# Where the convolution phases stand among the attention blocks: 15 ahead instead of 16, a first transform put behind the scores, three and two phases per attention step instead of two and one

## The chip, the core and the metric

The kernel runs on one core of a Trainium2 chip. The core has a matrix engine (PE, with its weight loads shown as PEld), a vector engine (DVE), a scalar engine (ACT), a general engine (POOL) and a queue engine (SP) that here only issues DMA transfers; POOL issues some as well. Each engine takes its instructions in a fixed order and waits at the head of its queue until what the head needs is there. The metric is the device time of one execution in microseconds (us). A change of less than 0.3% can hardly be told from none.

## What is computed

One layer of a diffusion backbone, in float32, on 1024 latent tokens and 256 context tokens. After a modulated normalisation one projection feeds two groups of heads: attention over a neighbourhood plus context keys, and a long convolution (Hyena) done by Fourier transforms. Both outputs are normalised, joined and put through one output projection; a convolutional feed-forward follows.

```python
proj = h @ w_in
q, k, v = ...                                  # 8 attention heads of width 64
a   = attend(q, k, v)                          # window + all context keys, one softmax
z   = x1 * _long_conv(v_h, k_f[:, 0], bias[0]) # Hyena: two convolutions in a row
hyo = x2 * _long_conv(z,   k_f[:, 1], bias[1])
x = x + g1 * (concat(rms(a), rms(hyo)) @ w_out)
u = dwconv3(h2 @ w_up); x = x + g2 * ((silu(gate) * up) @ w_down)
```

## The kernel before, in words

The program is one long stream, traced in Python and then put into an order for each engine by a scheduler, which takes instructions by priority (earlier traced is more urgent, and a block in `high_priority` more still) as their inputs become ready in its own estimate. The order is fixed when the kernel runs.

The stage that matters lies between the input projection and the output projection:

- **The convolution chains.** `chain(j)` is a generator for one block of 128 channels: blocks 0 to 3 are latent, block 4 is the context. It stops at eight `yield`s, four for each of the two convolutions `o`; what lies between two stops is a *phase*. Phase 0 is the forward transform: PE matmuls with `dftf` (L805), ACT scalings (L813 to L818) and DVE rotations (L819). Phase 1 is a butterfly (L826 to L831) and the product with the filter spectrum `K` (L844 to L847). Phase 2 is the inverse butterfly (L852 to L857) and rotations (ACT L862, L863, DVE L864). Phase 3 is the inverse transform (PE L877) and the gate (L882 to L884, or ACT L887 and DVE L888 to L890 in the second convolution), and in the second convolution the store of the result to `hyd` (L895, for the context block L898).
- **Two lanes.** Blocks 0, 2, 4 follow each other in lane 0, blocks 1 and 3 in lane 1. The list `turn2` says which lane gives the next phase: 0, 0, then 1 and 0 in turn. There are 40 phases in all. `phases(n)` traces the next n of them.
- **Ahead of the attention** 16 phases are traced with high priority: all eight of block 0, seven of block 1 and the first of block 2. They have three PSUM banks `cA`. Afterwards the chains have one bank, in the rest of the program.
- **The attention.** `attend(p_)` handles one pair of heads, four pairs in all. For each half `b` of the queries it computes the scores of two column blocks (PE L1068, DVE mask and maximum L1089, L1096, L1099, ACT exponentials L1102, L1103), stops, then sums (L1149), turns the weights around (PE L1112, copied out by ACT L1022 or DVE L1020), multiplies with the values (PE L1030) and normalises (PE L1040, L1045, DVE L1159). A pair stops three times. At the stops `phases(2)`, `phases(1)`, `phases(2)` are traced, and `phases(2)` at the end of a pair: five within a pair, seven with its end.
- **Bias tables** `tb` are filled by POOL's transfers (L967), 16 for each of three tables in each pair.
- **After the attention** `w_out` is loaded in nine pieces `wor` (L1205) into the memory that the chains leave, each split into a high and a low part (ACT L1197, DVE L1198), two or three pieces in flight. The attention output is split likewise (`ar`, ACT L1291, DVE L1292), the convolution output is read back as `y` (L1304), normalised (L1306, L1309), turned around (PE L1312) and split (`mr`, L1314, L1315). The output projection `psd` (L116 to L118, three matmuls for each product) takes `ar` for a block of 128 tokens first and `mr` after it, and the feed-forward follows.

Of the kernel before, what the change touches and what calls it, by code (L numbers as in the profile page):

```python
# [24 lines left out]
NH, DH = 8, 64  # L25
# [61 lines left out]
def _build(nc, tc, top, V, A, G, T, Q, I, O, dbg, upto):  # L87
# [20 lines left out]
    def bk(tag):  # L108
        pl, n, bufs = banks[tag]
        return pl.tile([P, 512 * n], F32, tag=tag, name="ps" + tag, bufs=bufs)  # L110
# [389 lines left out]
    with ies:  # L500
# [3 lines left out]
        for gi, (s, col, tl) in enumerate(groups):  # L504
            xs = []
# [24 lines left out]
            n = P * len(tl)  # L530
# [232 lines left out]
    dftf = cp.tile([P, 2, 256], F32, name="dftf")  # L763
    idft = cp.tile([P, 2, 2, P], F32, name="idft")
    with tc.high_priority(offset=2000):
        Q.dma_start(out=dftf.rearrange("p a b -> p (a b)"), in_=I["t_dft"].flatten().rearrange("(p x) -> p x", p=P))
        Q.dma_start(out=idft.rearrange("p a b c -> p (a b c)"), in_=I["t_idft"].flatten().rearrange("(p x) -> p x", p=P))

    S4B, TB = 3, 1
    CHP = 2000  # L770

    def chain(j):
# [22 lines left out]
        for o in range(2):  # L795
            uv = u.rearrange(v2, i=2)
            Gt = s8()
            Gv = Gt.rearrange(f4, h=2, i=2, q=4)
            for h in range(2):
                hs = slice(h * P, (h + 1) * P)  # L800
                for rp in range(2):
                    pa = bk("cA")
                    xs = slice(rp * 256, (rp + 1) * 256)
                    for i in range(2):
                        T.matmul(pa[:, i * 256:(i + 1) * 256], dftf[:, i, hs], uv[:, i, xs], start=True, stop=True)  # L805
                    pv = pa.rearrange("p (i r c) -> p i r c", i=2, r=2)
                    if not lat:
                        A.copy(Gv[:, h, :, 2 * rp:2 * rp + 2], pv)
                        continue
                    for ri in range(2):  # L810
                        r = 2 * rp + ri
                        if r == 0:
                            A.copy(Gv[:, h, :, 0], pv[:, :, 0])  # L813
                            continue
                        c, s, ns = tw_chain(h, r)
                        t = cp.tile([P, 2, P], F32, tag=f"t{b_}", name="t", bufs=TB)
                        A.activation(t[:, 0], pv[:, 1, ri], AF.Copy, scale=ns)
                        A.activation(t[:, 1], pv[:, 0, ri], AF.Copy, scale=s)  # L818
                        V.scalar_tensor_tensor(Gv[:, h, :, r], pv[:, :, ri], c, t, op0=ALU.mult, op1=ALU.add)  # L819
# [52 lines left out]
            for rp in range(2):  # L872
                pa = bk("cA")
                xs = slice(rp * 256, (rp + 1) * 256)
                for i in range(2):
                    for h in range(2):
                        T.matmul(pa[:, i * 256:(i + 1) * 256], idft[:, i, h], Ys[:, h, i, xs], start=h == 0,  # L877
                                 stop=h == 1, skip_group_check=True)
# [26 lines left out]
    def phases(n):  # L905
        for _ in range(n):
            if turn2:
                next(lanes[turn2.pop(0)], None)

    with tc.high_priority(offset=CHP):  # L910
        phases(16)
    cbk.close()
    cbk = Banks("bkd", "right", "tile", cA=(1, 1))
    for _ in ada:
# [137 lines left out]
    def attend(p_):  # L1052

        with tc.issue_after(blast0) if p_ == 1 else ExitStack():
            q, k = qkload(p_) if p_ else first
# [7 lines left out]
        hs = [slice(h * DH, (h + 1) * DH) for h in range(2)]  # L1063
        Pc = {}

        def smm(outs, qc, kc):
            for h in range(2):
                T.matmul(outs[h], q[hs[h], qc], kc(hs[h]), start=True, stop=True, tile_position=(DH * h, 0),  # L1068
                         skip_group_check=True)

        def scores(cb, l, l2, j):

            u0, u1 = BLK[cb]
            nu = u1 - u0
            a0 = 2 * cb - 1 + u0
            var = (0, 1, 1, 2)[cb]
            qc = [slice((2 * cb + half) * P, (2 * cb + half + 1) * P) for half in range(2)]
            m = [stat(f"m{h}") for h in range(2)]
            loc = [[], []]
            for half in range(2):  # L1080
                r0, nr = HALF_ROWS[half]
                n = nu * nr * 8
                sl = bk("S").rearrange("p (h x) -> p h x", h=2)
                smm([sl[:, h, :n] for h in range(2)], qc[half], lambda r: kg[r, a0:a0 + nu, r0 * 8:(r0 + nr) * 8])
                for h in range(2):
                    reg = Pring[h][cb][:, half, :, r0:r0 + nr].rearrange("p u r c -> p u (r c)")
                    loc[h].append(reg)
                    tv = tbs[var][:, HOFF[half]:HOFF[half] + nr * 64].rearrange("p (h u x) -> p h u x", h=2, u=4)[:, h]
                    V.tensor_tensor_reduce(out=reg, in0=sl[:, h, :n].rearrange("p (u x) -> p u x", u=nu),  # L1089
                                           in1=tv[:, u0:u1], op0=ALU.add, op1=ALU.max, scale=1.0, scalar=-3.0e38,  # L1090
                                           accum_out=m[h][:, half:half + 1])
            sc = bk("S").rearrange("p (h x) -> p h x", h=2)
            for half in range(2):
                smm([sc[:, h, half * 256:(half + 1) * 256] for h in range(2)], qc[half], lambda r: k[r, LT:])
            m2 = stat("n", 4)
            V.tensor_reduce(m2, sc.rearrange("p h (a x) -> p (h a) x", a=2), axis=AX.X, op=ALU.max, negate=True)  # L1096
            pc = tp.tile([P, 2, 2, 256], F32, tag="pc", name="pc", bufs=3)
            for h in range(2):
                V.scalar_tensor_tensor(m[h], m[h], -1.0, m2[:, 2 * h:2 * h + 2], op0=ALU.mult, op1=ALU.min)  # L1099
                for half in range(2):  # L1100
                    c = 4 * h + 2 * j + half
                    A.activation(loc[h][half], loc[h][half], AF.Exp, bias=m[h][:, half:half + 1], accum_out=l[:, c:c + 1])  # L1102
                    A.activation(pc[:, h, half], sc[:, h, half * 256:(half + 1) * 256], AF.Exp,  # L1103
                                 bias=m[h][:, half:half + 1], accum_out=l2[:, c:c + 1])
            Pc[cb] = pc
# [38 lines left out]
        for b in range(2):  # L1144
            l, l2 = stat("l", 8), stat("l2", 8)
            for j in range(2):
                scores(2 * b + j, l, l2, j)
            yield
            V.tensor_add(l, l, l2)  # L1149
            av = bk("av")  # L1150
            for j in range(2):
                cb = 2 * b + j
                for kt in range(2):
                    ps = turn(lambda h, i: Pc[cb][:, h, i, kt * P:(kt + 1) * P])
                    av_mm(av, 256 * j, vs[:, 10 + kt], ps, kt == 0)
                for vt, ps in local(cb):
                    av_mm(av, 256 * j, vt, ps, False)
            bs = recips(l, 8)
            V.tensor_mul(dst[:, 2 * b:2 * b + 2], av.rearrange("p (b r c) -> p b r c", b=2, r=16),  # L1159
                         bs.rearrange("p (b r c) -> p b r c", b=2, r=16))  # L1160
            if b == 0:
                yield
# [6 lines left out]

    for p_ in range(4):  # L1170
        for n, _ in enumerate(attend(p_)):
            phases(2 - n % 2)
        phases(2)
    ces.close()
    cbk.close()
# [407 lines left out]
    for f in range(NFF):  # L1583
# [7 lines left out]
        i, cs = f // 2, slice(f % 2 * 256, f % 2 * 256 + 256)  # L1591
# [132 lines left out]
    xs = {}  # L1724
# [107 lines left out]
```

## Time and profile before

| what | value |
|---|---|
| three runs | 1839.21, 1842.02 and 1844.18 us, median 1842.02 |
| the profiled execution, its own time | 1843.86 us |
| its span, from the first to the last instruction | 1841.9 us |
| busy share of the span: PE, DVE, ACT, POOL | 94%, 74%, 49%, 22% |
| mean granted PE clock | 0.964 of full speed |
| end of the last projection matmuls, start of the attention's scores | 562 us, 588 us |
| last normalisation of the attention (L1159) | 846.55 us |
| first matmul of the output projection | 861.32 us |

The profile is of one execution. A row of the timeline gives the start and the length of a group of equal instructions in us, the engine, the line of the kernel, what is written and read, and in brackets how long the engine had been idle before it and what ended that. The windows view gives for each stretch the busy time of PE, PEld, DVE, ACT and POOL with the count of instructions, the granted PE clock, the share of DMA time and the rate. The chain of waits follows the work that ended last back to its start. Busy times of PE overlap a little, as its matmuls are pipelined.

### The profile page before, as it was taken

What the parts mean: (1) busy time and instruction counts of PE and PEld (TensorE: products, weight loads), DVE (VectorE), ACT (ScalarE), POOL (GpSimd) and SP (SyncE); (2) the same over time, 40 slices, a digit from 0 to 9 for tenths busy, and PEclk for the clock granted to TensorE, in tenths of its full rate; (3) what the DMA queues carried; (4) which work ended last, traced back from release to release, by engine and by line L of the source; (5) the groups of instructions that cost most, each with busy time, mean ns of one, the idle gap of its engine ahead of it and who ended that gap; (6) DMA issues with size and microseconds to landing.
All of it is one profiled execution on the core that took longest, in us unless ns stands there. A gap on an engine that the chain in (4) does not pass through costs nothing.

```text
span 1841.9 us, 27359 instructions
## 1 busy us (share of the span) xinstructions
PE 1725.3 (94%) x9999; PEld 1453.2 (79%) x9999; DVE 1367.1 (74%) x2166; ACT 893.9 (49%) x1852; POOL 396.7 (22%) x487
## 2 busy tenths in 40 slices
PE   5899999999996898898997999999999999999997
PEld 1588788788884455566886999999999999888786
DVE  4658957853778798973558798889777877566797
ACT  4645535533334566664556444444444444443452
POOL 2266565674117442600110000000000000000001
PEclk7899999999997799998998999999999999999999
DMA  7424354356546332516231554454222123934653
GB/s 247 157 87 135 105 176 131 112 132 192 168 143 194 96 106 69 147 35 213 78 109 50 165 167 151 157 164 163 82 65 73 60 65 102 350 112 142 207 185 132
DMA packets 202440, 249.78 MB, mean 136 GB/s; under 512 B 21923, under 2 KB 147988, under 8 KB 202050
## 3 DMA queue, kind: packets, MB, share of 16 engines
q1 hardware_dynamic: 190360, 230.75, 38.8%
q0 software_dynamic: 10240, 16.46, 3.7%
q8 instruction: 79, 1.29, 0.3%
q10 hardware_dynamic: 1705, 0.82, 0.2%
q14 instruction: 56, 0.45, 0.1%
HBM read 176.75 MB, written 71.20 MB: 135 GB/s over the span
## 4 chain that ended last, share of the span: by engine, by line
PE 38%; DVE 14%; DMA 8%; issue 4%; ACT 3%; POOL 1%; DVEq 0%; POOLq 0%; ACTq 0%; SPq 0%
PE psd L116 6%; PE psd L117 6%; PE psd L118 6%; PE psa L116 3%; PE psa L117 3%; PE psa L118 3%; DMA wt<-in_w_down_dram 2%; PE psc L118 2%; PE psc L117 2%; PE psc L116 2%; PE psb L117 2%; PE psb L118 2%; PE psb L116 2%; DMA tdr<-wt 2%; POOL tb L967 1%
## 5 line engine op out<-in xcount | busy, mean ns | idle before, releaser
L116 PE MATMUL psp<-hh,wh 128*128 128x512 f32 (+1 forms) x552 | 200.6, 363 | 1.9 <-ACT wh L121 1.9
L118 PE MATMUL psp<-hh,wl 128*128 128x512 f32 (+1 forms) x552 | 199.5, 362 | 1.0 <-POOL wl L122 1.0
L117 PE MATMUL psp<-hl,wh 128*128 128x512 f32 (+1 forms) x552 | 198.9, 360 | 0.0
L1747 POOL TENSOR_TENSOR rs<-rs,mhalf 128x1 f32<-128x1 f32 x10 | 7.7, 776 | 816.0 <-DVE rs L1746 816.0
L116 PE MATMUL psa<-T,ws 128*128 128x256 f32 (+1 forms) x528 | 166.0, 314 | 3.9 <-ACT rows L1546 2.7
L117 PE MATMUL psa<-T,ws 128*128 128x256 f32 (+1 forms) x528 | 165.3, 313 | 0.0
L118 PE MATMUL psa<-T,ws 128*128 128x256 f32 (+1 forms) x528 | 164.7, 312 | 0.0
L116 PE MATMUL psd<-wd,gs 128*128 128x512 f32 x360 | 140.8, 392 | 3.1 <-ACT gs L121 3.1
L117 PE MATMUL psd<-wd,gs 128*128 128x512 f32 x360 | 141.0, 392 | 0.0
L118 PE MATMUL psd<-wd,gs 128*128 128x512 f32 x360 | 123.3, 390 | 1.7 <-DVE gs L122 1.6
L116 PEld LDWEIGHTS psp<-hh,wh 128*128 128x128 f32 x552 | 104.9, 190 | 23.2 <-issue 7.4
L118 PEld LDWEIGHTS psp<-hh,wl 128*128 128x128 f32 x552 | 104.9, 190 | 16.4 <-POOL wl L122 1.2
L117 PEld LDWEIGHTS psp<-hl,wh 128*128 128x128 f32 x552 | 104.8, 190 | 14.1 <-issue 0.4
L116 PE MATMUL psc<-T,ws 128*128 128x384 f32 (+1 forms) x352 | 110.1, 313 | 5.8 <-ACT ws L121 5.8
L118 PE MATMUL psc<-T,ws 128*128 128x384 f32 (+1 forms) x352 | 110.0, 313 | 0.3 <-DVE ws L122 0.3
L967 POOL DMA_DIRECT2D tb<-rpw x192 | 100.5, 531 | 45.1 <-DVE m L1089 31.7
L117 PE MATMUL psc<-T,ws 128*128 128x384 f32 (+1 forms) x352 | 110.1, 313 | 0.0
L117 PE MATMUL psb<-T,ws 128*128 128x384 f32 (+1 forms) x352 | 109.4, 311 | 0.0
L118 PE MATMUL psb<-T,ws 128*128 128x384 f32 (+1 forms) x352 | 109.4, 311 | 0.0
L116 PE MATMUL psb<-T,ws 128*128 128x384 f32 (+1 forms) x352 | 109.2, 310 | 0.0
L116 PEld LDWEIGHTS psa<-T,ws 128*128 128x128 f32 x528 | 101.4, 192 | 5.7 <-ACT rows L1546 4.0
L117 PEld LDWEIGHTS psa<-T,ws 128*128 128x128 f32 x528 | 101.3, 192 | 0.0
(405 smaller groups left out, 4785.8 us busy)
## 6 DMA issues: line engine op xcount, KB each, us to landing
wada<-in_w_ada_dram SPq DMA_DIRECT2D x48, 512.0 KB
wr<-in_w_up_dram SPq DMA_DIRECT2D x44, 512.0 KB
gr<-gdr SPq DMA_DIRECT2D x44, 320.0 KB
wr<-in_w_in_dram SPq DMA_DIRECT2D x23, 512.0 KB
wt<-in_w_down_dram SPq DMA_DIRECT2D x44, 256.0 KB
tdr<-wt SPq DMA_DIRECT2D x44, 256.0 KB
gdr<-cv SPq DMA_DIRECT2D x22, 512.0 KB
wr<-tdr SPq DMA_DIRECT2D x20, 512.0 KB
```

Source lines behind the costliest of these rows:

```text
L116: T.matmul(out, ah, bh, start=start, stop=False, skip_group_check=True)
L117: T.matmul(out, ah, bl, start=False, stop=False, skip_group_check=True)
L118: T.matmul(out, al, bh, start=False, stop=stop, skip_group_check=True)
L967: blast[0] = G.dma_start(out=tv[:, :, a * 8:a * 8 + 64], in_=rpw[var, :, 2 * p_:2 * p_ + 2, :, d * 8:d * 8 + 64].rearrange("q h u x -> q ( ...
L1747: G.tensor_tensor(rs, rs, mhalf, op=ALU.pow)
```

## The change

Three edits. `phases(16)` ahead of the attention becomes `phases(15)`, so the first phase of block 2 is traced within the attention, without high priority and on the single bank. A list `gate` holds the last scores matmul of the newest half block; from then on, each forward transform of a chain's first convolution (`o == 0`) is put behind that matmul in PE's order, by a constraint on the order that adds no semaphore. And the stops of a pair trace 3, 2 and 3 phases instead of 2, 1 and 2: eight within a pair where there were five, ten with its end where there were seven. 25 phases are left for the attention, so they are used up at the second stop of the third pair.

```diff
+    gate = []
@@ chain(j), phase 0
-                    for i in range(2):
-                        T.matmul(pa[:, i * 256:(i + 1) * 256], dftf[:, i, hs], uv[:, i, xs], start=True, stop=True)
+                    with tc.issue_after(gate[0]) if gate and o == 0 else ExitStack():
+                        for i in range(2):
+                            T.matmul(pa[:, i * 256:(i + 1) * 256], dftf[:, i, hs], uv[:, i, xs], start=True, stop=True)
@@
     with tc.high_priority(offset=CHP):
-        phases(16)
+        phases(15)
@@ smm, the scores matmuls
-                T.matmul(outs[h], q[hs[h], qc], kc(hs[h]), start=True, stop=True, tile_position=(DH * h, 0),
-                         skip_group_check=True)
+                smm.last = T.matmul(outs[h], q[hs[h], qc], kc(hs[h]), start=True, stop=True,
+                                    tile_position=(DH * h, 0), skip_group_check=True).ins
@@ attend, behind the scores of a half
+            gate[:] = [smm.last]
             yield
@@
         for n, _ in enumerate(attend(p_)):
-            phases(2 - n % 2)
+            phases(3 - n % 2)
         phases(2)
```

No instruction is added or taken away; what changes is where they stand. In the changed kernel a line number is two higher from the transform (L805 becomes L807) and three higher behind the gate (L1159 becomes L1162, L1205 becomes L1208).

The first place is PE's queue where the attention begins, behind the transposes of the cached keys (L732). Before, the eight transform matmuls of block 2 (L805) stand first, and the last phase of block 1 (L877) stands among the scores (L1068):

```order
L732 MATMUL pstB<-ident,ck 128x128 x2
L805 MATMUL pscA<-s_5771,dftf 128x256 x8
L1068 MATMUL psS<-k,q 128x264 x2
L1068 MATMUL psS<-k,q 128x288 x2
L877 MATMUL pscA<-s_5623,idft 128x256 x4
L1068 MATMUL psS<-k,q 128x256 x4
L1068 MATMUL psS<-k,q 128x352 x2
L877 MATMUL pscA<-s_5623,idft 128x256 x4
L1112 MATMUL psX<-ident,pc 128x128 x6
```

In the changed kernel the scores follow at once, and no chain matmul stands before the second block's last scores:

```order
L732 MATMUL pstB<-ident,ck 128x128 x2
L1070 MATMUL psS<-k,q 128x264 x2
L1070 MATMUL psS<-k,q 128x288 x2
L1070 MATMUL psS<-k,q 128x256 x4
L1070 MATMUL psS<-k,q 128x352 x2
L1114 MATMUL psX<-ident,pc 128x128 x6
...
L1070 MATMUL psS<-k,q 128x256 x4
L807 MATMUL pscA<-s_5969,dftf 128x256 x4
```

So the transform of block 2 moved behind the scores of the first half block, and the last phase of block 1, which shares its bank, moved behind that.

The second place is DVE at the same point. Before, the rotations of block 2 (`s_5773`), its butterfly and half of the rotations of block 1 (`s_5623`) stand ahead of the first mask (L1089, written as ISA):

```order
L819 SCALAR_TENSOR_TENSOR s_5773<-pscA,tw,t 128x2x128
L826 TENSOR_TENSOR s_6035<-s_5773 128x1024
L864 SCALAR_TENSOR_TENSOR s_5623<-s_5623,tw,t 128x2x128
L827 TENSOR_TENSOR s_5773<-s_5773 128x4x256
L830 TENSOR_TENSOR s_6036<-s_6035 128x4x128
L831 TENSOR_TENSOR s_6036<-s_6035 128x4x128
L1089 ISA Pl_5833,m_5950<-psS,tb_5857 128x3x88
```

In the changed kernel only rotations of block 1 are left there, and the maxima of the attention follow:

```order
L866 SCALAR_TENSOR_TENSOR s_5623<-s_5623,tw,t 128x2x128 x4
L1091 ISA Pl_5792,m_5909<-psS,tb_5816 128x3x88
L1091 ISA m_5909 128x1
L1091 ISA Pl_5796,m_5910<-psS,tb_5816 128x3x88
L1091 ISA m_5910 128x1
L866 SCALAR_TENSOR_TENSOR s_5623<-s_5623,tw,t 128x2x128 x2
L1098 TENSOR_REDUCE n<-psS 128x4
```

So all that block 2 had DVE do there has moved behind the first masks.

The third place is ACT's queue behind the attention. Before, the splits of all nine pieces of `w_out` stand ahead of the split of the attention output (L1291), mixed with the attention's last copies:

```order
L1197 ACTIVATE wh_8309<-wor,vec 128x1024
L1222 ACTIVATE sq<-at_5828 128x1024
L1197 ACTIVATE wh_8315<-wor,vec 128x1024
L1197 ACTIVATE wh_8321<-wor,vec 128x1024
L1197 ACTIVATE wh_8327<-wor,vec 128x512 x2
L1291 CAST ar<-at_5828 128x512 x2
```

In the changed kernel the last copies of the last chain phase (L889, before L887) stand behind all of the attention, and the attention output is split after four pieces:

```order
L1225 ACTIVATE sq<-at_5787 128x1024
L889 COPY tt<-pscA 128x256 x2
L1200 ACTIVATE w_8280<-wor,vec 128x1024 x2
L1200 ACTIVATE w_8281<-wor,vec 128x1024
L1200 ACTIVATE wh_8303<-wor,vec 128x1024
L1294 CAST ar<-at_5787 128x512 x2
L1200 ACTIVATE wh_8309<-wor,vec 128x1024
```

So the chains now end last in this stage, and the output projection needs four pieces instead of nine before it can begin. On SP's queue the reads of `y` (L1307) have likewise moved ahead of the last pieces of `wor`, behind the seventh of the nine.

## The prediction

> **What bounds the kernel now.** I read the windows view first. Its columns are the stretch, its length, the busy time of PE, PEld, DVE, ACT and POOL with their counts, the granted PE clock, the DMA share and GB/s.
>
> ```profile
> 576.40:618.00 41.60, 22.31 (x68) 13.93 (x68) 39.46 (x70) 16.93 (x61) 24.20 (x45) 0.66 0.74 214
> 631.60:846.50 214.90, 197.10 (x1227) 120.47 (x1228) 176.79 (x376) 140.73 (x433) 71.42 (x134) 0.98 0.34 96
> 640.00:680.00 40.00, 38.46 (x248) 23.25 (x246) 38.56 (x78) 26.82 (x85) 13.63 (x26) 1.00 0.39 112
> 861.30:900.00 38.70, 38.68 (x166) 31.28 (x167) 15.54 (x33) 17.06 (x33) 3.81 (x7) 0.93 0.48 164
> 1003.00:1600.00 597.00, 583.95 (x3823) 575.31 (x3823) 482.75 (x668) 267.76 (x425) 0.36 (x9) 0.99 0.40 129
> ```
>
> The limit changes from stage to stage. Where the attention begins (576 to 618) DVE binds: 39.46 of 41.60 us, with PE half idle. In the attention (631.6 to 846.5) PE is busy 91.7% of the time and DVE 82%; in its dense piece (640 to 680) both stand at 96%. Behind it PE binds alone (38.68 of 38.70, later 97.8%), so a shift of the output projection's start reaches the end unless a later wait takes it up. Next the chain of waits at the two seams (start, length, what).
>
> ```profile
> 577.37 5.65 DMA s<-lxd
> 583.07 2.09 PE pscA L805 x4
> ...
> 827.60 0.70 DVE s L890
> 828.32 2.78 DMA hyd<-s
> ...
> 831.17 3.40 DMA wor<-in_w_out_dram
> ...
> 861.32 0.79 PE psd L116
> ```
>
> At the first seam the end hangs on a load for block 2's transform. At the second it hangs on the **last gate of the chains**, L890: it lets `hyd` be stored and the memory for `w_out` go free. The attention's last row (L1159, at 846.55) is not on this chain.
>
> **The change, part one: the lead at the first seam.** The timelines of PE and DVE there:
>
> ```profile
> 575.82 0.64 PE L732 MATMUL pstB<-ident,ck 128*128 128x128 f32 x2
> 583.07 5.50 PE L805 MATMUL pscA<-s,dftf 128*128 128x256 f32 x16 [6.61 <-DMA s<-lxd]
> 588.49 1.20 PE L1068 MATMUL psS<-k,q 64*128 64x264 f32 x8
> ...
> 616.96 2.05 PE L805 MATMUL pscA<-s,dftf 128*128 128x256 f32 x4 [0.97 <-DMA s<-lxd]
> 618.93 1.12 PE L1030 MATMUL psav<-pt,vs 128*64 128x256 f32 x4
> ```
>
> ```profile
> 588.31 0.68 DVE L857 TENSOR_TENSOR s<-s 128x512 f32<-128x512 f32 x1
> ...
> 590.66 0.48 DVE L864 SCALAR_TENSOR_TENSOR s<-s,tw,t 128x256 f32<-128x256 f32 x1
> ...
> 591.91 0.48 DVE L864 SCALAR_TENSOR_TENSOR s<-s,tw,t 128x256 f32<-128x256 f32 x1 [0.16 <-ACT t L863]
> ...
> 598.07 0.42 DVE L1089 CUSTOM_DVE_ANT_0 Pl<-psS,tb 128x264 f32<-128x264 f32 x1
> ...
> 609.52 0.23 DVE L1099 SCALAR_TENSOR_TENSOR m<-m,n 128x2 f32<-128x2 f32 x2
> ...
> 631.60 0.17 DVE L1149 TENSOR_TENSOR l<-l,l 128x8 f32<-128x8 f32 x1 [0.66 <-ACT pc L1103]
> ```
>
> The first scores move from behind L805 to behind L732 and are done near 578 (576.46 plus 1.20). DVE isn't free then: it still has block 1's butterfly, whose last row L857 ended at 588.99, some 0.8 earlier without two rotations of block 2 ahead of it: 588.2. Four L864 follow, 1.25 apart because ACT paces them (590.66, 591.91): about 4.3 us with the first wait, so the first mask starts near **592.5** instead of 598.07. To the first maximum (L1099) there stand four masks of 0.44, one L1096 of 1.2 (the shape of L844 below) and two L864 at 1.25, which is 5.5: 598 instead of 609.52. The exponentials begin 0.2 later. Before, from L1099 to the first product with the values (618.93) it was 9.4 us, of which L805 and its wait held 2.9 (0.97, then 616.96 to 618.93); 6.5 puts that product at 604.5, **14.4** us earlier. From there to the sums (L1149) the eight matmuls that now stand behind the scores take 2.2 (rate below): a lead of **12** us at L1149, about 619.5 for 631.60.
>
> **Part two: what was put off.** The lead isn't free: what DVE and PE did for the chains before 631.6 now comes later.
>
> ```profile
> L844 DVE TENSOR_TENSOR s<-s,K 128x1024 f32<-128x1024 f32 x13 | 15.8, 1218 | 1.5 <-DMA K<-Kd 0.6 <-DMA K<-Kc 0.5 <-ACT s L808 0.3
> L864 DVE SCALAR_TENSOR_TENSOR s<-s,tw,t 128x256 f32<-128x256 f32 x30 | 14.4, 478 | 5.6 <-ACT t L863 5.3
> L847 DVE TENSOR_TENSOR s<-s,s 128x512 f32<-128x512 f32 x14 | 9.5, 682 | 0.0
> L888 DVE TENSOR_TENSOR s<-tt,pscA 128x256 f32<-128x256 f32 x9 | 3.8, 417 | 4.9 <-ACT tt L887 4.9
> L1198 DVE SCALAR_TENSOR_TENSOR w<-wor,vec,w 128x1024 fp32r<-128x1024 f32 x3 | 3.9, 1285 | 3.3 <-ACT w L1197 3.3
> ```
>
> (The lines view: group, count, busy us, mean ns, idle before it.) Counted in DVE's order up to the first L1149, before against after, the change puts off 13 rotations (7 L819, 6 L864) at 0.478, 8 rows of 128x1024 at 1.218 (L826, L827, L844, L845, L852, L853), 14 of 128x512 at 0.682 (L828 to L831, L846, L847, L854 to L857, L890) and 4 gate rows at 0.417: 6.2 + 9.7 + 9.5 + 1.7 = **27.1 us of DVE**. PE puts off 20 L805 and 16 L877; the windows view for these lines alone gives the rates.
>
> ```profile
> 618.00:847.20 229.20, 21.57 (x79) 13.25 (x77) 0.97 0.32 91
> 618.00:847.20 229.20, 24.63 (x96) 17.82 (x96) 0.97 0.32 91
> ```
>
> 0.273 and 0.257 us each: 5.5 + 4.1 = **9.6 us of PE**. The stage then holds 197.1 + 9.6 = 206.7 us of PE. For DVE 5.2 of its 176.8 were four splits of `w_out` (L1198, these three and one of another name, at 1.285), which the changed order puts behind the attention: 176.8 - 5.2 + 27.1 = 198.7. From 619.5, at the old 91.7% PE takes 225.4 (last L1159 at 844.9); at the 96% of the dense piece 215.3 (834.8). DVE would be at 88% to 92%. The stage gets denser since the three-phase stops leave DVE and PE more to choose from, but two engines that both pass 90% wait for each other more. I take 94%: 219.9, so the last L1159 starts at **839.4**, 7 us before its old place. Of the lead of 12 us, 5 go to work that was put off.
>
> The single bank adds waits: the transform of block 2 holds it and block 1's last phase stands behind, where three banks were before. In the attention all chain phases were on this one bank already, and its cost is in the 91.7%. POOL's tables come by its own queue and only their due time moves 6 to 12 us earlier; if a first table were late, the lead would shrink by that much (the range has it).
>
> **Part three: the end of the chains.** In the changed order ACT and DVE have the chains' last gates behind the last L1159, and PE seven of the last eight L877 behind the last product.
>
> ```profile
> 824.43 1.89 PE L877 MATMUL pscA<-s,idft 128*128 128x256 f32 x8
> 826.41 0.37 ACT L887 COPY tt<-pscA 128x256 f32<-128x256 f32 x1 [2.30 <-PE pscA L877]
> 827.60 0.69 DVE L890 TENSOR_TENSOR s<-s,s 128x512 f32<-128x512 f32 x1
> 843.34 1.15 ACT L1197 ACTIVATE wh<-wor,vec 128x1024 fp32r<-128x1024 f32 x1 [1.03 <-DMA wor<-in_w_out_dram]
> 846.55 0.69 DVE L1159 TENSOR_TENSOR at<-psav,bs 128x512 f32<-128x512 f32 x1 [0.75 <-ACT bs L1047]
> 847.67 1.04 ACT L1222 ACTIVATE sq<-at 128x1024 f32<-128x1024 f32 x1
> 860.66 1.12 ACT L1291 CAST ar<-at 128x512 fp32r<-128x512 f32 x2
> 870.87 0.63 ACT L1306 ACTIVATE jk<-y 128x512 bf16<-128x512 f32 x1 [9.09 <-DMA y<-hyd]
> ```
>
> ```profile
> 861.32 0.79 PE L116 MATMUL psd<-w,ar 128*128 128x512 f32 x1 [1.12 <-ACT ar L1291]
> 881.47 0.40 PE L116 MATMUL psd<-wh,mr 128*128 128x512 f32 x1
> ```
>
> The last L890 ended at 828.29, 18.3 **before** L1159. Now it comes behind: L1159 0.69, L1222 1.04 on ACT, then two gates, each L887 to L890 1.88 long (826.41 to 828.29), with the second group of L877 (1.89 for all eight) partly between: 5 to 7 us, I take 6.6. The chains end at 839.4 + 6.6 = **846**, 17.7 later than before. What hung on them keeps its distances: the store of `hyd` and the first load 2.9 us behind the end, the fourth piece's ACT split 15.05 behind it (843.34 against 828.29). In the changed order the split of the attention output (L1291) stands behind the fourth piece instead of the ninth: 846 + 15.05 + 1.15 = 862.2, and L116 0.66 behind it, as before (860.66 to 861.32): **862.8**, 1.5 late. This reordering pays for nearly all of the 17.7, since five splits no longer stand ahead. The products with `mr` need `y`. Its load was issued with L1291's start, 860.66, and landed 10.2 later (870.87), `mr` was used 10.6 behind that (881.47). The load now goes ahead of the last two pieces on SP; it lands at 846 + 29 to 30, `mr` is ready near 886, 4.5 late, while PE would arrive at 862.8 + 20.15 = 883. So the projection is late by 1.5 to 4.5; I take 3, for PE finds products with `ar` of further token blocks in part of that gap. If `w_out`'s pieces come at the old 6 us spacing throughout, 4.5 is the end that holds.
>
> **Sum.** The profiled execution took 1843.86 us (span 1841.9) and is 1.84 above the median of 1842.02. 1843.86 + 3 = 1846.9, or on the median **1845.0**: +0.16%, which is no change, since about 0.3% (5.5 us) is what a measurement of this kernel can tell from none.
>
> **The rivals.** *Faster*: the whole stage runs at the dense piece's 96%, as chain work fills each wait of PE. Then L1159 is at 834.8, the chains end near 841 and psd starts 4.6 before the forecast, at 858, with `mr` ready at 881: -3 on psd. With the full lead of 14.4 kept it is 5.4; a share of 98% (210.9 us) would make it 10. I take 6: about **1836**. For it speaks that DVE's idle 38 us (214.9 - 176.8) exceed the 22 net added; against it, that no long stretch shows 96% on both.
>
> *Slower*: the put-off work is hidden nowhere, and the one bank makes the chain's phases follow each other. It decides once the stage's PE share falls under 91.7%: at 90% the 206.7 us take 229.7, L1159 is at 849.2, the chains end at 856, `mr` is ready at 896 and psd's start is 11.5 late. Since some of that is the gap which 3 already counts, +8 to +12: about **1852**.
>
> *The clock*: in 576 to 618 PE was granted 0.66, with idle stretches of 6.6 and more ahead of L805.
>
> ```profile
> 623.20 1.13 PE L805 MATMUL pscA<-s,dftf 128*128 128x256 f32 x4
> ```
>
> Four L805 took 2.05 at 616.96 and 1.13 here. In the changed seam PE has nothing from 578 to 592.5, so the transposes and products from 598 to 608 may all run at the long price: six groups that lose 0.4 to 0.9 each, +2 to +5, with a later end of the chains: about **1849**. The Trainium skill, "TensorE: Matmul & The Clock Gate", section "HAM oscillation — how this bites in real kernels", says that PE idle for more than about 3.4 us falls to half its clock and pays again after each such wait. By that rule the longer gap of the change costs something of its own. The trace agrees in kind (2.05 against 1.13 for the same four), but shows the price in the old seam too, so most of it is paid already.
>
> That the change doesn't do what it says is excluded by the order of the instructions: PE's scores do stand directly behind L732.
>
> **How the numbers follow.** My forecast, within 5.5 us of the old time, has 0.43 as the two ends of part three and the 94% lie in it; *faster* 0.25; *slower* 0.20; *the clock* 0.12. The two last are slower by over 0.3%: 0.32. The range takes the faster case to 1834 (its 1836 with 2 us of spread) and the slower one to 1856 (1852 and the upper 12 of its price, plus 2): about 0.2 lies outside.
>
> **What the changed profile would show.** The first mask near 592.5 and the first sums near 619.5 (part one); the windows view from there to the last L1159 with a PE share of 94% and DVE near 90% (part two); the last L890 behind the last L1159 by 6 us, the first `wor` load 2.9 us later, the first L116 of psd near 863 and the first with `mr` near 886 (part three). Wrong it would be if the first sums came later than 626 (no lead), if the PE share were under 91.7% or over 96%, or if the projection started over 6 us away from 861.3.

## The result, and the profile after

| | before | changed |
|---|---|---|
| median (us) | 1843.1 (4 runs, 1839.21 to 1846.95) | 1863.97 (4 runs, 1862.4 to 1865.13) |
| ratio | | 1.0105, 95% interval 1.0086 to 1.0125 |
| first sums (L1149, now L1152) | 631.60 | 619.32 |
| last normalisation of the attention (L1159, now L1162) | 846.55 | 856.20 |
| end of the last gate of the chains (L890, now L892) | 828.29 | 863.73 |
| first matmul of the output projection | 861.32 | 880.28 |

The kernel is slower by 1%; no change was forecast. The windows view of the changed kernel, for the stretches that the prediction spoke of (columns as there):

```profile
576.00:618.00 42.00, 20.88 (x84) 9.56 (x82) 20.85 (x49) 15.71 (x53) 22.40 (x42) 0.62 0.49 138
619.30:856.20 236.90, 206.51 (x1254) 127.23 (x1252) 194.60 (x409) 143.58 (x456) 71.13 (x133) 0.97 0.31 84
880.30:919.00 38.70, 37.10 (x157) 29.62 (x158) 20.43 (x37) 20.47 (x35) 4.26 (x7) 0.95 0.60 203
```

At the seam DVE has 20.85 us of work where it had 39.46. In the attention stage the work is about what the prediction counted (206.51 us of PE, 206.7 forecast; 194.60 of DVE, 198.7 forecast), but it takes 236.9 us: PE's share is 87%, not 94%. The seam itself went nearly as forecast. PE's timeline there:

```profile
574.13 0.66 PE L732 MATMUL pstB<-ident,ck 128*128 128x128 f32 x2 [0.41 <-DMA ck<-in_cache_ctx_k_dram]
574.73 2.21 PE L1070 MATMUL psS<-k,q 64*128 64x264 f32 x8
591.13 2.08 PE L1070 MATMUL psS<-k,q 64*128 64x256 f32 x8 [14.20 <-DVE m L1091]
...
609.39 1.14 PE L1070 MATMUL psS<-k,q 64*128 64x256 f32 x8
610.46 1.13 PE L807 MATMUL pscA<-s,dftf 128*128 128x256 f32 x4
613.10 1.13 PE L807 MATMUL pscA<-s,dftf 128*128 128x256 f32 x4 [1.51 <-DVE s L821]
...
623.12 1.86 PE L807 MATMUL pscA<-s,dftf 128*128 128x256 f32 x4
...
627.50 1.03 PE L807 MATMUL pscA<-s,dftf 128*128 128x256 f32 x4
...
635.38 1.99 PE L879 MATMUL pscA<-s,idft 128*128 128x256 f32 x8
...
655.54 1.13 PE L807 MATMUL pscA<-s,dftf 128*128 128x256 f32 x4 [1.34 <-DMA s<-lxd]
```

and DVE's:

```profile
590.19 0.43 DVE L1091 CUSTOM_DVE_ANT_0 Pl<-psS,tb 128x264 f32<-128x264 f32 x1
...
595.14 0.28 DVE L1101 SCALAR_TENSOR_TENSOR m<-m,n 128x2 f32<-128x2 f32 x2
604.27 0.69 DVE L1022 COPY pt<-psX 128x512 f32<-128x512 f32 x1 [8.86 <-PE psX L1114]
...
619.32 0.17 DVE L1152 TENSOR_TENSOR l<-l,l 128x8 f32<-128x8 f32 x1 [2.96 <-ACT pc L1105]
...
856.20 0.69 DVE L1162 TENSOR_TENSOR at<-psav,bs 128x512 f32<-128x512 f32 x1 [1.01 <-ACT bs L1049]
...
863.04 0.69 DVE L892 TENSOR_TENSOR s<-s,s 128x512 f32<-128x512 f32 x1
```

Three things are to be seen. PE stands idle for 14.20 us before the second scores, and DVE for 8.86 us behind the first maxima: before, PE did the transform of block 2 about there, and DVE its first rows. The transform now starts at 610.46 instead of 583.07, right behind the scores matmul that gates it, and its four groups of four take 18 us from first to last, where the same 16 in a row took 5.50 us on three banks. The last phase of block 1 (L879) follows on the same bank at 635 instead of 594, and the next transform starts at 655.5 instead of 617.0: the chains are by then **38.6 us** behind, against 27.4 at the gate. They make up only 3 of these: their end is 35.4 us late. Rows of the chain of waits, at the seam and at the end:

```profile
588.04 2.09 DMA tb<-rpw
590.19 0.43 DVE Pl L1091
591.13 2.09 PE psS L1070 x8
...
859.80 1.98 PE pscA L879 x8
861.85 0.38 ACT tt L889
862.25 0.42 DVE s L890
862.68 0.34 DVE s L891
863.04 0.70 DVE s L892
863.76 2.78 DMA hyd<-s
866.62 3.38 DMA wor<-in_w_out_dram
870.14 1.16 ACT w L1200
```

The last gate, the store of `hyd` and the loads of `w_out` hold the projection, which starts 16.55 us behind the chains' end. The attention had been done for 7 us when the chains ended. It still had a small part in that end: in PE's order six of the eight matmuls of the last inverse transform's first half stand behind the attention's last rows, and they come 3.8 us after the first two.

```profile
852.54 0.60 PE L879 MATMUL pscA<-s,idft 128*128 128x256 f32 x2
...
856.92 1.54 PE L879 MATMUL pscA<-s,idft 128*128 128x256 f32 x6
```

Of the 21.3 us between the two profiled executions 19.0 are there at the projection's start; behind it PE waits 1.60 us for `mr` (at 901.52).

### The profile page after: what moved, and what is told of

The parts are those of the page before. It is cut to its first block, busy times and chain, and to the rows that moved or that the text cites. A ratio compares the mean times of both kernels' runs of the same rounds, so it can differ in the third digit from the quotient of the medians.

```text
span 1863.3 us, 27344 instructions
## 1 busy us (share of the span) xinstructions
PE 1721.8 (92%) x9999; PEld 1450.8 (78%) x9999; DVE 1365.3 (73%) x2166; ACT 893.4 (48%) x1852; POOL 396.1 (21%) x487
## 4 chain that ended last, share of the span: by engine, by line
PE 52%; DVE 21%; DMA 11%; ACT 7%; issue 6%; POOL 3%; SPq 0%; DVEq 0%; POOLq 0%; ACTq 0%
PE psd L116 5%; PE psd L118 5%; PE psd L117 5%; PE psp L116 4%; PE psp L118 4%; PE psp L117 4%; DMA wt<-in_w_down_dram 3%; PE psa L116 2%; PE psa L117 2%; PE psa L118 2%; DMA tdr<-wt 2%; PE psc L117 2%; PE psc L118 2%; PE psc L116 2%; PE psb L117 1%
```

## The experiments

Two theories were set against each other. **A**: the chains have a pace of their own on their single PSUM bank, so they end a fixed time after block 2's transform starts, and that end holds the projection. **B**: the work put off at the seam loads PE and DVE more than the stage bears, wherever it stands. All kernels ran beside the kernel before; ratios are to it, with 95% intervals. The table is read from the timelines, one execution each: start of block 2's transform, end of the last gate, the time between, the last normalisation of the attention, and the start of the projection. Before, e7 and e9 have the same chains and the same attention; in their three executions the transform, the chains' end and the last normalisation stand some 4 us apart, with 245 us between transform and chains' end in each. So a few us from one kernel to another mean nothing in those columns.

| kernel | transform | chains end | between | attention's last | projection | ratio |
|---|---|---|---|---|---|---|
| before | 583.1 | 828.3 | 245 | 846.5 | 861.3 | 1 |
| changed | 610.5 | 863.7 | 253 | 856.2 | 880.3 | 1.0105 |
| e1, no gate | 580.3 | 829.9 | 250 | 848.9 | 865.3 | 1.0028 [1.0015, 1.0040] |
| e2, gate later | 628.6 | 871.7 | 243 | 832.8 | 888.3 | 1.0165 [1.0143, 1.0186] |
| e3, two banks | 615.1 | 816.2 | 201 | 971.9 | 984.4 | 1.0659 [1.0636, 1.0683] |
| e4, gate at first scores | 585.9 | 836.8 | 251 | 854.9 | 867.5 | 1.0016 [1.0002, 1.0030] |
| e5, 16 phases with gate | 584.6 | 831.0 | 246 | 857.9 | 869.6 | 1.0058 [1.0034, 1.0081] |
| e6, gate at first block | 594.8 | 849.2 | 254 | 860.6 | 875.8 | 1.0084 [1.0061, 1.0108] |
| e8, stops alone | 583.0 | 831.1 | 248 | 858.6 | 870.4 | 1.0040 [1.0025, 1.0055] |
| e10, more DVE rows | 582.3 | 841.6 | 259 | 853.1 | 867.6 | 1.0062 [1.0041, 1.0084] |
| e11, fewer DVE rows | 581.1 | 824.5 | 243 | 854.2 | 866.7 | 1.0039 [1.0023, 1.0054] |

**e1, the gate taken out** of the changed kernel:

```diff
-            gate[:] = [smm.last]
+            pass
```

> The gate is left out; 15 phases ahead and the three- and two-phase stops stay. Theory A (the chains have a pace of their own on their single bank, and their end follows the start of block 2's transform): the transform starts near 583 us again, as soon as its load lands, but with one bank it takes longer than the 5.5 us of before, so the second transform comes some 13 us later than before (630 for 617), the chains end near 841 and the output projection starts near 858 to 862: 1838 to 1846 us. Theory B (the work put off at the seam loads PE and DVE more than they can bear, wherever it stands): the vector engine is full at the seam again, 1843 us within 4. If 15 phases or the stops were the cause and not the gate: above 1855 us.

The transform starts at 580.3, the chains end at 829.9, and 0.8 of the 1.05% are gone. So most of the cost comes with the gate; the 15 phases matter since they put block 2's transform behind it, and without the gate they and the stops cost 0.28% together. A's time was missed all the same, and B's too. The fear for the single bank was too large (the second transform starts at 616.0, not at 630, and the chains end 11 us earlier than A had it), but now the attention ended last, at 848.9, and the projection started 16.4 us behind it.

**e2, the gate moved on** to the scores of the pair's second half:

```diff
-            gate[:] = [smm.last]
+            if b or p_:
+                gate[:] = [smm.last]
-            phases(3 - n % 2)
+            phases(3 - n % 2 if p_ or n > 1 else 0)
```

> The gate of the first head pair is moved to the last scores of its second half, and the first two stops hand out nothing. The same work, put off by some 25 to 30 us more. Theory A: block 2's transform starts near 638 us instead of 610, the chains end by as much later (near 890), the projection's first matmul near 906, and the time is 1887 to 1895 us. Theory B: only 10 us more of DVE work stand behind the second sums than in the changed kernel; 1868 to 1875 us.

```profile
832.81 0.69 DVE L1163 TENSOR_TENSOR at<-psav,bs 128x512 f32<-128x512 f32 x1 [1.54 <-ACT bs L1049]
...
870.98 0.69 DVE L892 TENSOR_TENSOR s<-s,s 128x512 f32<-128x512 f32 x1
```

(DVE's timeline of e2.) The sharpest of the runs: the attention ends 23 us **earlier** than in the changed kernel and 14 earlier than before, and yet this kernel is the slowest of the three, since its projection starts 16.6 us behind the chains' end, as in the changed kernel. By its time alone (1875.04 us) B would have it: A forecast 1887 to 1895. But A's transform was put 10 us too late (628.6 came, 638 was forecast), and the chains then took 243 us instead of 253; and a stage that can't bear its load would have shown in a late attention. What e2 shows is that the chains' end holds the projection, with the attention done 39 us earlier. That the distance from the transform to that end is fixed holds only within some 10 us, and partly by luck, as its steps aren't fixed:

```profile
813.31 1.03 PE L807 MATMUL pscA<-s,dftf 128*128 128x256 f32 x4
...
848.19 1.10 PE L807 MATMUL pscA<-s,dftf 128*128 128x256 f32 x4 [1.47 <-DVE tt L885]
```

(PE's timeline of e2.) The attention ended between these two transforms, and the step took 34.9 us, where before and the changed kernel took 51.1 and 48.1 for the same step. The last step, from there to the chains' end, took 23.5 us with no attention beside it, against 25.5 and 23.8. So the attention does slow the chains on the way, but not in their last step.

**e3, a second bank for the chains**, taken from the attention's turned weights:

```diff
-    cbk = Banks("bkd", "right", "tile", cA=(1, 1))
+    cbk = Banks("bkd", "right", "tile", cA=(1, 2))
-    abk = Banks("bk2", "left", "tile", av=(1, 1), S=(2, 2), X=(1, 2))
+    abk = Banks("bk2", "left", "tile", av=(1, 1), S=(2, 2), X=(1, 1))
```

> The changed kernel with two PSUM banks for the chains, and one instead of two for the attention's turned weights. The transform of block 2 starts as late as in the changed kernel. Theory A: the chains step faster, transforms follow each other after 30 us or less instead of 38 to 45, the chains end before 845 us, and the projection starts before 862: 1845 us or less, though the attention itself is slowed somewhat. Theory B: the put-off work is unchanged and a bank is taken away from the attention: 1864 us or more.

```profile
815.54 0.69 DVE L892 TENSOR_TENSOR s<-s,s 128x512 f32<-128x512 f32 x1
...
971.94 0.69 DVE L1162 TENSOR_TENSOR at<-psav,bs 128x512 f32<-128x512 f32 x1 [4.67 <-ACT bs L1049]
```

(DVE's timeline of e3.) Half of it came as forecast: the chains took 201 us instead of 253, with a start as late as in the changed kernel. The other half failed badly: the attention, with one bank for its turned weights, ended 116 us later, and the time is 6.6% up. So the chains step faster with a second bank beside a slower attention; as that also left the engines emptier, how much of the 52 us is the bank's own stays open.

**e4, the gate behind the first scores matmul**, and **e6, behind the first of the two blocks of a half**:

```diff
 e4, in scores(), behind the first smm
+                if half == 0 and j == 0:
+                    gate[:] = [smm.last]
 e6, behind scores() of a block
+                if j == 0:
+                    gate[:] = [smm.last]
 both
-            gate[:] = [smm.last]
```

> The gate is the first scores matmul of the newest half instead of the last one; everything else as in the changed kernel. The scores still come at once behind the key transposes, but block 2's transform fills the 14 us that PE is idle behind them. Theory A: the transform starts between 583 and 592 us, the second one near 630, the chains end near 842 with the attention about as early as in the changed kernel at the first sums plus 3 to 6 us: 1836 to 1844 us. Theory B: the vector engine is nearly full at the seam again (99 us of chain work left at the first sums in its order, 96 before, 120 in the changed kernel): 1840 to 1848 us.

> The gate is the last scores matmul of the first of the two column blocks of a half, instead of the second. Theory A: block 2's transform starts near 593 us, between before (583) and the changed kernel (610); the chains end 243 to 253 us later, at 836 to 846, the projection starts 16 to 17 us behind that or 13 to 16 behind the attention's end, whichever is later, at 858 to 864: 1841 to 1848 us. If the time followed the number of chain rows left behind the first sums (104 us of DVE, 96 before, 120 changed), it would be a third of the way, 1850 us.

The chains did nearly as A has it (ends at 836.8 and 849.2, where it had 842 and 836 to 846), but now the attention came last, at 854.9 and 860.6, later than the 846.5 of before, and it held the projection: 12.7 and 15.1 us ahead of it. Both times are above what A forecast; that of e4, some 1846 us by its ratio, lies where B had it. In e4 the first sums even came at 635.6, behind those of before: with the transform let in between the scores, the lead was gone.

**e5, 16 phases again, gate and stops kept**, so that the gate acts on blocks 3 and 4 only, and **e8, the stops alone** on the kernel before:

```diff
 e5, on the changed kernel
-        phases(15)
+        phases(16)
 e8, on the kernel before
-            phases(2 - n % 2)
+            phases(3 - n % 2)
```

> 16 phases ahead again, gate and new stops kept: block 2's first transform is traced ahead of the attention on three banks and before any gate exists, so the gate acts on the first transforms of blocks 3 and 4 alone. Theory A (the chains' end follows the start of block 2's transform by 243 to 253 us): transform near 583 us, chains end between 826 and 836, projection 861 to 866, 1842 to 1848 us. If the gate on the later blocks had been part of the cost, or the stops: above 1852 us.

> The kernel before with the three- and two-phase stops alone (16 phases ahead, no gate). The chains start as before and keep their pace: they end between 826 and 836 us. Theory: what the attention loses is the DVE time of the chain rows that stand within it, one for one. In DVE's order 10.6 us of chain rows stand between the sixth and the seventh sums, where before has 6.1 (and the run with 16 phases and the gate 13.7): that step takes 27 to 28 us instead of 23.1, the last normalisation comes at 848 to 853, the projection 15 us later, and the time is 1844 to 1850 us. If the stops do nothing to the time: 1843.

The time of e5 came out above what A gave it, where the other case had put it (above 1852). Transform and chains are as before in both, the attention is not: it ends at 857.9 and 858.6, some 12 us late. The time of e8 was met, but by luck: its step from the sixth to the seventh sums took 31.7 us (27 to 28 expected), the attention ended later than the 848 to 853 expected, and the projection followed it by 11.8 us instead of 15. So the stops cost 0.4% by themselves where nothing else holds the chains; that the gate on blocks 3 and 4 costs anything beyond that is not shown, as the intervals of e5 and e8 overlap. In the changed kernel the stops cost nothing and bring nothing: with the old two- and one-phase stops it has the same rows in the same order on all five engines. (Argued, not shown: the gate and the single bank keep the chains behind anything that the stops could hand out.)

**e10 and e11** ask whether the attention's end is simply set by the DVE time of the chain rows in its stage. In the kernel before these rows add up to 108 us between the first sums and the last L1159, in the changed one to 131; the stage grew by 22.0.

```diff
 e10
-                V.tensor_mul(B, Xs[:, h, ::-1], ki)
+                for _ in range(2 if j > 2 else 1): V.tensor_mul(B, Xs[:, h, ::-1], ki)
 e11
-                V.tensor_sub(Ys[:, h, 0], Ys[:, h, 0], B[:, 0])
-                V.tensor_add(Ys[:, h, 1], Ys[:, h, 1], B[:, 1])
+                if j < 3: V.tensor_sub(Ys[:, h, 0], Ys[:, h, 0], B[:, 0])
+                if j < 3: V.tensor_add(Ys[:, h, 1], Ys[:, h, 1], B[:, 1])
```

> The kernel before, in which blocks 3 and 4 do their first product with the filter spectrum twice (the second time over the same result): 8 more rows of 128x1024, 9.2 us of DVE, all within the attention stage. If the attention's end takes up DVE time of the chains one for one: last L1159 8 to 10 us later (855), projection 15 us behind it, 1850 to 1853 us. If PE bounds the stage, as the prediction had it, with DVE at 82%: the added rows are hidden but for 2 us, 1843 to 1845 us.

> The kernel before without the two rows that finish the product with the filter spectrum in blocks 3 and 4 (the cross terms are left out): 16 rows of 128x512 fewer, 9.8 us of DVE, all within the attention stage. One for one: last L1159 8 to 10 us earlier (838), the chains end earlier as well, and the projection starts 9 to 10 us earlier: 1833 to 1835 us, or 1837 if the reads of the convolution output then come last. If PE bounds the stage: 1841 to 1843 us.

```profile
853.08 0.69 DVE L1159 TENSOR_TENSOR at<-psav,bs 128x512 f32<-128x512 f32 x1 [0.61 <-ACT bs L1047]
```

```profile
854.25 0.69 DVE L1159 TENSOR_TENSOR at<-psav,bs 128x512 f32<-128x512 f32 x1 [0.50 <-ACT bs L1047]
```

(DVE's timeline of e10, then of e11.) More rows made it later by 6.5 us, roughly in keeping with one for one. Fewer rows made it later **as well**, by 7.7 us. The theory of one for one falls. Both edits also let the scheduler draw another order of attention and chain rows, on PE and ACT too. The order that e11 drew must have cost more than the 9.8 us of work taken out; no run holds the order fixed, so this is argued.

**e7 and e9** ask what the tail is worth, on the kernel before: the tail is reordered as the changed kernel has it.

```diff
 e7: the four pieces of the attention half, then ar, then the rest
+    for k in range(4):
+        wo_load(k, None)
...
+    for k in range(4, 6):
+        wo_load(k, att_split.last)
+    for n in range(2):
+        ylast = Q.dma_start(out=ypre[n], in_=hyd[ORDER[n]]).ins
+    for k in range(6, KC):
+        wo_load(k, att_split.last, ylast)
 e9, besides: the token scales
-            for i in range(a, b):
-                for t in (asq, sq):
+            for t in (asq, sq):
+                for i in range(a, b):
```

> The kernel before, with its chains and attention as they were; only the tail is reordered as the changed kernel has it: the split of the attention output stands behind the fourth piece of w_out and the reads of the convolution output go ahead of the last three. If the projection's start is set by the later of the chains' end plus 16.6 us (828.3 gives 845) and the attention's end plus the split (846.5 + 0.7 + 1.0 + 1.2 + 0.7 = 850), it starts near 850 instead of 861.3; the convolution half must then be ready by 871 instead of 881.5, which the earlier reads allow if they land by 860. 1833 us; 1838 if the convolution half is late by 5. If something else held the projection (the load of the later pieces), 1843 as before.

```profile
842.85 0.69 DVE L1159 TENSOR_TENSOR at<-psav,bs 128x512 f32<-128x512 f32 x1 [0.74 <-ACT bs L1047]
```

```profile
852.51 1.14 ACT L1295 CAST ar<-at 128x512 fp32r<-128x512 f32 x2 [7.88 <-PE psX L1232]
```

(Timelines of e7, DVE and ACT.) The order came out as meant, and the gain didn't: 0.9988 [0.9975, 1.0001]. The split of the attention output now waits 7.88 us for the matmuls of the token scales (L1232, 30 of them in 7.1 us), which the expectation had left out. The projection starts 12.3 us behind the attention instead of 14.8.

> The reordered tail of the run before this on the kernel before, and the 16 matmuls of the token scales that read the first three pairs' squares now stand ahead of those that need the last pair's (30 matmuls of 0.23 us each held the split of the attention output 7 us behind the attention's end, since it reuses the memory that they read). Eight of them, 1.9 to 3.7 us, move under the wait for the last squares. The projection should start 8 to 9 us behind the last normalisation instead of 12.2, at 855 or less in a profile whose normalisation stands at 846: 1836 to 1840 us. If the split waits for something else: 1841 as in that run.

0.9987 [0.9976, 0.9998], and the projection 11.9 us behind the attention: the earlier matmuls didn't start earlier, since they stood behind a wait for DVE's read of the same bank (L1235, 0.25 us idle at 843.53, then 16 in a row of 3.90 us). In this kernel the token scales are not those of the reference; the edit takes the sums of the early and the last pairs in turn within one bank. So no run beats the kernel before by more than about 0.1%.

## Why the prediction was wrong, step by step

**The lead (part one) came out, in part by luck.** First mask 590.19 (592.5 forecast), first sums 619.32 (619.5). The mask came 2.3 us early, but in this execution the key transposes (L732) already stood 1.7 us early (574.13 instead of 575.82). From mask to sums it then took 29.1 us where 27.0 were forecast. The three executions with the order of before have their first sums between 627.8 and 631.6, so an agreement within 0.2 us says little. The lead couldn't have been much larger: the bias table for the first mask landed at 590.13 (588.04 and 2.09), just ahead of the mask. So the clock rival isn't excluded: of its 2 to 5 us, up to 2 may lie in these 29.1. PE was granted 0.62 over the seam against 0.66. The Trainium skill, "TensorE: Matmul & The Clock Gate", section "HAM oscillation — how this bites in real kernels", says that a wait of PE of more than about 3.4 us brings it back to half its clock; the trace agrees in kind: behind 14.20 us of idle PE the eight scores at 591.13 took 2.08 us, those at 609.39 took 1.14. The former lie on the chain of waits, so about 1 us was paid there, little beside the 17.5 us below.

**The work put off (part two) was right as a count and wrong in its effect.** PE's 206.51 us of work were forecast at 206.7. The term that failed is the share: 94% was chosen, 87% measured (206.51 of 236.9). It put the attention's end 16.8 us too early (839.4 for 856.20), and with it the chains' end, which the prediction hung on that row; in the prediction's own sum 17 of the 17.5 us by which the projection started later than forecast (880.28 for 862.8) are this. The reason given, that the three-phase stops leave the engines more to choose from, was empty: the stops move no row here. Two of the prediction's own signs of being wrong came: a share under 91.7%, and a projection more than 6 us away from 861.3.

**What stood in its place.** PE's share was the wrong quantity. The stage is two dependent streams that share in-order queues, and they end at different times:

- The chains run from the start of block 2's transform to their end in 243 to 259 us in the ten kernels that keep a single bank from there on, though the start moves by 48 us and the attention's end by 28 (table; in five of them the first transform still has three banks). The gate delayed that start by 27.4 us, the second transform came 38.6 late, and 35.4 remained. The 11 us between aren't the single bank's alone: e1 has the same bank, and its second transform comes 35.7 us behind the first, against 45.1 in the changed kernel and 33.9 before. In the changed kernel the first transform stands among the attention's scores. This step was in the trace of before: 583.07 to 828.29, with transforms at 617, 657, 701, 752 and 803; the changed kernel has them at 656, 694, 737, 792 and 840, all 36 to 40 us later.
- The attention's end depends on the order that the scheduler draws. Eight of the nine other orders on the usual banks end it between 848.9 and 860.6; the ninth, e2, where the chains stood back, at 832.8. That of before, 846.5 (842.4 and 842.8 in e9 and e7, which share it), is at the early end. Of the 22.0 us by which the stage grew in the changed kernel, 9.4 are more work of PE (206.51 for 197.10), and 12.6 more idle time. The lines of PE show where most of that lies:

```profile
L1032 PE MATMUL psav<-pt,vs 128*64 128x256 f32 x364 | 55.4, 399 | 9.7 <-ACT pt L1024 5.7 <-DVE pt L1022 2.9 <-DVE at L1141 0.9
L879 PE MATMUL pscA<-s,idft 128*128 128x256 f32 x98 | 27.2, 423 | 1.8 <-DVE s L891 1.6
L807 PE MATMUL pscA<-s,dftf 128*128 128x256 f32 x88 | 25.0, 409 | 4.4 <-DVE tt L885 1.6 <-DMA s<-lxd 1.3 <-DVE n L1098 1.0
```

```profile
L1030 PE MATMUL psav<-pt,vs 128*64 128x256 f32 x364 | 56.9, 409 | 3.0 <-DVE pt L1020 2.1 <-ACT pt L1022 0.5
L877 PE MATMUL pscA<-s,idft 128*128 128x256 f32 x96 | 24.6, 393 | 0.6 <-DVE s L846 0.6
L805 PE MATMUL pscA<-s,dftf 128*128 128x256 f32 x68 | 18.3, 392 | 0.0
```

(The lines view of PE from the first sums to the last normalisation, 619.3 to 856.2 us of the changed kernel, then 631.6 to 846.5 of before; the last figures are idle time ahead of these rows.) 6.2 us of PE are lost directly ahead of chain matmuls, 0.6 before. 6.7 more are lost ahead of the products with the values, which wait for the copies of the turned weights on ACT and DVE. What makes these copies late is open: that chain rows stand ahead of them is likely, but e11 shows that the DVE time of the chain rows alone doesn't decide.

No run met the time that A gave it, as A left out that the attention's end can hold the projection too. What the runs bear out of A is the near constant time of the chains, and that their end holds the projection where it comes last (changed, e2).

**The tail (part three) was right in its distances.** The chains ended 7.5 us behind the start of the last normalisation (6.6 forecast), the projection started 16.55 behind that (16.8), the `mr` products at 901.52, 21.2 behind the projection's start. But that the chains' end follows the attention's last row held here by the order alone (the six matmuls above) and isn't a rule: in e2 the two are 39 us apart. The projection starts at the later of two times: the chains' end plus 16.6 (changed, e2) or the attention's last row plus 12 to 16 (all others). By the attention alone the changed kernel's would have started at 868 to 873; the chains made it 880.3. And the chains' end, on which the prediction saw the kernel before hang, had more slack than it knew: e7 shows that the nine pieces ahead of the split held only some 2.5 us, and the attention's end the rest.

**The rivals.** *Slower* had the right direction and the right sign (a share under 91.7%), with too small a price: 90% of PE where 87% came, 1852 where 1864 came. Its reason, that the put-off work is hidden nowhere, doesn't fit e2, where more was put off and the attention ended earlier. With the start of the transform in hand, the result could have been worked out without a share: 610 for the transform, plus the 245 us of before, plus 16.8, is 872 for the projection, 11 us late. The other 8 us to 880 are the chains' 253 us instead of 245, which nothing in the trace of before foretold.

## What to carry to other kernels

Where two streams share engines in a fixed order, read each stream's pace first: follow its repeated step (here the transforms) through the trace, and move it as a whole by what its first step is delayed. Here that was good to about 10 us in 250, with single steps off by more. A busy share of one engine says how much room there is, not who can use it. A wait that fills an idle engine is worth removing only if what filled it isn't the head of the longer stream, and the buffers that the head had at its old place (three banks here) are given up with it. In e1 that alone cost the second transform some 2 us.

## What the runs showed that was not expected

- Reordering costs by itself. Making work less (e11) or the stops wider (e8) changed the drawn order and cost 0.4% each, with no chain started later.
- The bank of the turned weights is worth more here than a second one for the chains: with one instead of two the attention ended 116 us later than in the changed kernel, while the chains gained 52.
- In e7 the 30 matmuls of the token scales, with two output columns each, took 7.1 us on PE, about 0.24 us each at a granted clock of 0.58, and held the split of the attention output. Eight of the same matmuls just ahead of them, from 842.66 to 843.71, took 0.13 us each at a granted clock of 1.00.
